# Layer 1's gate and up products by Strassen's algorithm, with one block of each pair run ahead for one half of the tokens

## The chip, the cores and the metric

One NeuronCore of a Trainium2 chip. TensorE (PE) multiplies, VectorE (DVE), ScalarE (ACT) and GpSimdE (POOL) work on tiles in on-chip memory, SyncE (SP) and ScalarE issue DMA transfers. The metric is the device time of one execution in microseconds. The kernel before: median 2474.93 us of 3 runs (2474.85 to 2480.22).

## The reference

A trunk of four residual layers over 1024 tokens of width 1024, in float32: a gMLP and pooling mixer, a SwiGLU ffn, RWKV-7 time mixing, a SwiGLU ffn, and a last norm. The change touches the last two:

```python
def wkv7_scan(r, w, k, v, a, b):        # 16 heads of 64 x 64 state, one step per token
    def step(state, inp):
        r_t, w_t, k_t, v_t, a_t, b_t = inp
        sa = jnp.einsum('bhvk,bhk->bhv', state, a_t)
        state = (state * w_t[:, :, None, :] + sa[..., None] * b_t[:, :, None, :]
                 + v_t[..., None] * k_t[:, :, None, :])
        return state, jnp.einsum('bhvk,bhk->bhv', state, r_t)

# in rwkv7_time_mix, on the scan's output y of each head:
mean = jnp.mean(y, axis=-1, keepdims=True)
var = jnp.mean(jnp.square(y - mean), axis=-1, keepdims=True)
y = ((y - mean) * lax.rsqrt(var + GN_EPS)).reshape(bsz, seq, d)
y = y * ln_w.astype(f32) + ln_b.astype(f32)
...
return (y * g) @ w_o, v_first

def swiglu(hn, w_gate, w_up, w_down):    # gate, up: 1024 x 2816, down: 2816 x 1024
    return (jax.nn.silu(hn @ w_gate) * (hn @ w_up)) @ w_down

h = h + swiglu(rms_norm(h, ffn_norm[layer]), ffn_w_gate[layer], ffn_w_up[layer], ffn_w_down[layer])
```

## The kernel before, in words

**Numbers.** A float32 matrix product is made of three float32r products of high and low parts: `mm3` issues hi x hi, lo x hi and hi x lo (lines 344 to 346) into one PSUM tile. Every dense matmul is 128x128 by 128x512. `split` makes the two parts: ScalarE copies to hi (line 143), VectorE subtracts for lo (line 144).

**Tiling.** Activations are transposed, features on partitions, in two halves of the tokens, A and B, of 512 each. The ffn's width of 2816 is 22 blocks of 128. For a block, gate and up take 8 steps of K times 3 matmuls each, 24, and so does down (8 output tiles). A unit of work in the text is 24 matmuls.

**Weights.** `push` writes the list of weight blocks (0.5 MB each) in the order of use; `take` hands out the next, and issues the load of the following ones on ScalarE's DMA queue into `raw` (3 tiles), and splits them into `whi` and `wlo` (3 tiles each).

**Order.** The Tile framework's scheduler sets the order of every engine's instructions from a timeline of its own; it is fixed when the program is built, and each engine then goes through its list in order. `drive(dense, side, ratio)` lets two generators of work go along: for each unit of the dense one the side one gets `ratio` of its own costs, at a priority that is `AHEAD` (450) instructions ahead. `beside` does the same for the projections.

**Layer 1.** For half A, then B: the projections (`project_gate`, `project`), the recurrence `recur(h)`, the output projection `out_proj`, the ffn. Recurrence (1), that of half B, runs beside the ffn of half A. `recur` goes through 8 chunks of 64 tokens. `burst` is one chunk: `below2` (sm<-XT,w), `own` (sm<-uv,gt, copied by ScalarE to akv), the product with the state (sm<-S,ar), the Gram products of the next chunk (`gram`, sm<-ar,bk, masked by VectorE to gt), sm<-Q,XT (copied to uv by ScalarE and VectorE), yp<-S,ar, sm<-uv,bkt with the new state S, yp<-uv,gt, then `flip_bk` of the next chunk (sm<-ident,bk, copied by ScalarE to bkt) and its `below` (sm<-XT,gt, copied by ScalarE and VectorE to w). bk has one tile, ar and uv two. `ordered` keeps the recurrence's TensorE instructions in the order written. After each second chunk `post` takes the pair's output yp: statistics (VectorE), rsqrt (GpSimd, line 349), 16 ScalarE instructions that scale yp into ysb, VectorE and GpSimd half each of the layer norm, eight transposes (sm<-ident,ysb) and eight VectorE products with the gate gch, which go to memory as y_d.

**What runs beside and after it.** `BESIDE` and `G1A` split half A's 22 ffn blocks: 2 beside `project_gate`, 16 (48 units with ratio 3.0) for recurrence (1), then 2 with the loads of y_d, the output projection of half B, `norm_split` of B (which makes B's normalised activations), the last 2 of A, and B's 22 blocks. `final_down` ends each half with the last norm and the transposes back.

## Time and profile before

| what | value |
|---|---|
| median of 3 runs | 2474.93 us (2474.85 to 2480.22) |
| profiled execution | 2477.63 us |
| its span, first to last instruction | 2475.9 us |
| TensorE busy | 2406.4 us, 97% |
| VectorE, ScalarE, GpSimd busy | 1382.7, 912.1, 244.6 us |
| DMA | 310.69 MB, mean 125 GB/s |
| recurrence (1) | about 1657 to 1870 us |
| half A's rest, y_d loads, output projection of B | 1870 to 2020 us |
| the rest of the ffn | 2020 to 2440 us |

Times inside an execution are microseconds from its first instruction. A group's row has line, engine, operation, output<-inputs by the program's names, shape and count, then busy time and mean nanoseconds of one, then the engine's idle time just before them with what ended most of it. PEld is the load of weights into TensorE, beside PE. Matmuls overlap, so their single durations add up to more than the time that they take. In a timeline a bracket gives the idle time ahead of an instruction and what released it.

### The profile page before, as it was taken

To read this page: it belongs to the slowest core of one execution; us is meant where nothing else is said; L and a number is where in the kernel's file an instruction comes from. 1 tells how busy PE (TensorE), PEld (TensorE's weight loads), DVE (VectorE), ACT (ScalarE), POOL (GpSimd) and SP (SyncE) were. 2 spreads that over 40 slices of the span, in tenths; PEclk is the share of its full clock that TensorE was granted. 3 is DMA by queue.
4 is the path that set the end of the run, shared out by engine and by line. 5 is a ranking of instruction groups with operands and counts; after the bars stand their busy time and mean duration, and the time that the engine had idled before them with its cause. 6 is when DMAs were issued, how large, how long until landed. Compare 5 with 4: busy or idle time off the path is not lost.

```text
span 2475.9 us, 37980 instructions
## 1 busy us (share of the span) xinstructions
PE 2406.4 (97%) x15735; PEld 1977.5 (80%) x15735; DVE 1382.7 (56%) x2126; ACT 912.1 (37%) x1369; POOL 244.6 (10%) x262
## 2 busy tenths in 40 slices
PE   8999999999999998999999999989999999999998
PEld 7888888888878787888878777778878778888887
DVE  6445634444875874655548847856555446444443
ACT  6233422222664432432325754433232324322223
POOL 0200000000014400211000133201111000000001
PEclk9999999999999999999999999999999999999999
DMA  5123433323355577542434465695444322433231
GB/s 179 49 60 89 150 102 102 119 86 94 109 176 139 140 208 202 156 127 70 135 112 143 153 168 134 191 234 140 119 128 128 111 85 75 147 102 118 87 98 56
DMA packets 436396, 310.69 MB, mean 125 GB/s; under 512 B 93376, under 2 KB 395584, under 8 KB 435456
## 3 DMA queue, kind: packets, MB, share of 16 engines
q10 hardware_dynamic: 297280, 210.53, 28.6%
q1 hardware_dynamic: 138944, 97.75, 13.8%
q8 instruction: 123, 2.02, 0.3%
q14 instruction: 49, 0.40, 0.1%
HBM read 254.68 MB, written 53.54 MB: 124 GB/s over the span
## 4 chain that ended last, share of the span: by engine, by line
PE 82%; DMA 6%; DVE 5%; ACT 2%; issue 2%; POOL 2%; SPq 0%; ACTq 0%; POOLq 0%; DVEq 0%
PE mm L344 22%; PE mm L345 22%; PE mm L346 22%; PE sm L1176 5%; DMA raw<-y_d 1%; DVE wlo L144 1%; PE yp L1176 1%; DMA raw<-in_ffn_w_down_dram 1%; DMA lnw<-in_rwkv_ln_w_dram 1%; ACT whi L143 1%; PE aux L1097 1%; PE mm L511 1%; PE mm L512 1%; PE mm L513 1%; PE aux L1098 1%
## 5 line engine op out<-in xcount | busy, mean ns | idle before, releaser
L345 PE MATMUL mm<-alo,whi 128*128 128x512 f32 x1952 | 766.7, 393 | 0.9 <-issue 0.8
L346 PE MATMUL mm<-ahi,wlo 128*128 128x512 f32 x1952 | 765.4, 392 | 1.7 <-DVE wlo L144 1.7
L344 PE MATMUL mm<-ahi,whi 128*128 128x512 f32 x1952 | 765.8, 393 | 0.8 <-ACT whi L143 0.8
L143 ACT ACTIVATE whi<-raw 128x1024 fp32r<-128x1024 f32 x288 | 304.6, 1059 | 744.7 <-PE mm L345 605.3
L144 DVE TENSOR_TENSOR wlo<-raw,whi 128x1024 fp32r<-128x1024 f32 x288 | 359.1, 1248 | 289.5 <-ACT whi L143 270.1
L346 PEld LDWEIGHTS mm<-ahi,wlo 128*128 128x128 f32 x1952 | 367.7, 188 | 82.5 <-issue 3.5
L345 PEld LDWEIGHTS mm<-alo,whi 128*128 128x128 f32 x1952 | 367.7, 188 | 79.9 <-issue 2.9
L344 PEld LDWEIGHTS mm<-ahi,whi 128*128 128x128 f32 x1952 | 367.7, 188 | 79.0 <-issue 2.1
L344 PE MATMUL mm<-hidhi,wdhi 128*128 128x512 f32 x624 | 240.5, 395 | 8.1 <-DVE h L424 3.8
L345 PE MATMUL mm<-hidlo,wdhi 128*128 128x512 f32 x624 | 245.0, 393 | 0.4 <-DVE hidlo L674 0.4
L346 PE MATMUL mm<-hidhi,wdlo 128*128 128x512 f32 x624 | 244.9, 392 | 0.0
L424 DVE TENSOR_TENSOR h<-h,mm 128x512 f32<-128x512 f32 x192 | 129.3, 686 | 149.7 <-PE mm L346 148.5
L143 ACT ACTIVATE wdhi<-raw 128x1024 fp32r<-128x1024 f32 x82 | 86.4, 1057 | 249.7 <-DMA raw<-in_ffn_w_down_dram 164.4
L144 DVE TENSOR_TENSOR wdlo<-raw,wdhi 128x1024 fp32r<-128x1024 f32 x82 | 100.2, 1223 | 112.1 <-ACT wdhi L143 112.0
L670 DVE TENSOR_TENSOR sg<-sg,mm 128x512 f32<-128x512 f32 x88 | 60.3, 686 | 157.1 <-PE mm L346 155.3
L344 PEld LDWEIGHTS mm<-hidhi,wdhi 128*128 128x128 f32 x624 | 117.5, 189 | 36.8 <-DVE h L424 6.4
L345 PEld LDWEIGHTS mm<-hidlo,wdhi 128*128 128x128 f32 x624 | 117.8, 189 | 25.7 <-DVE hidlo L674 1.3
L346 PEld LDWEIGHTS mm<-hidhi,wdlo 128*128 128x128 f32 x624 | 117.8, 189 | 24.9
L424 DVE TENSOR_TENSOR hA<-hA,mm 128x512 f32<-128x512 f32 x72 | 48.8, 686 | 77.2 <-PE mm L346 77.0
L349 POOL TENSOR_TENSOR nrs<-nrs,small 128x4 f32<-128x4 f32 x8 | 10.0, 1244 | 667.2 <-DVE nrs L371 667.2
L674 DVE TENSOR_TENSOR hidlo<-sg,hidhi 128x512 fp32r<-128x512 f32 x88 | 65.7, 748 | 10.0 <-ACT hidhi L673 10.0
L344 PE MATMUL mm<-xhi,whi 128*128 128x512 f32 (+1 forms) x160 | 65.3, 408 | 0.0
(299 smaller groups left out, 2886.3 us busy)
## 6 DMA issues: line engine op xcount, KB each, us to landing
raw<-in_ffn_w_gate_dram ACTq DMA_DIRECT2D x88, 512.0 KB
raw<-in_ffn_w_up_dram ACTq DMA_DIRECT2D x88, 512.0 KB
raw<-in_ffn_w_down_dram ACTq DMA_DIRECT2D x88, 512.0 KB
raw<-in_ab_w_in_dram ACTq DMA_DIRECT2D x16, 512.0 KB
raw<-in_ab_w_out_dram ACTq DMA_DIRECT2D x16, 512.0 KB
raw<-in_rwkv_w_r_dram ACTq DMA_DIRECT2D x16, 512.0 KB
raw<-in_rwkv_w_k_dram ACTq DMA_DIRECT2D x16, 512.0 KB
ar_d<-ar SPq DMA_DIRECT2D x16, 512.0 KB
```

The costliest lines, as they stand in the source:

```text
L143: act.activation(hi, src, AF.Copy)
L144: (eng or dve).tensor_tensor(out=lo, in0=src, in1=hi.bitcast(F32), op=ALU.subtract)
L344: pe.matmul(o, whi, xhi, start=first, stop=False)
L345: pe.matmul(o, whi, xlo, start=False, stop=False)
L346: pe.matmul(o, wlo, xhi, start=False, stop=last)
L424: dve.tensor_tensor(out=H[h][:, m, :], in0=H[h][:, m, :], in1=o, op=ALU.add)
L511: pe.matmul(ops[j], xhi[:, k, sl], whi[:, kk], start=(k == 0), stop=False)
L512: pe.matmul(ops[j], xhi[:, k, sl], wlo[:, kk], start=False, stop=False)
L513: pe.matmul(ops[j], xlo[:, k, sl], whi[:, kk], start=False, stop=(k == KT - 1))
L670: dve.tensor_tensor(out=s, in0=s, in1=o, op=ALU.mult)
L674: dve.tensor_tensor(out=lo, in0=s, in1=hi.bitcast(F32), op=ALU.subtract)
L1176: i = f(*args, **kw)
```

## The change

For layer 1's gate and up, a pair of column blocks (2i, 2i+1) with the two halves of K (rows of the weight) and the two halves of the tokens is a 2 x 2 by 2 x 2 block product. It is done with seven products of quarters where eight stood (Winograd's form of Strassen's algorithm); a quarter product is 4 steps of K, 12 matmuls. VectorE makes the sums of weights (`weights` in `full_steps`) and of activations (`combine`), and adds up the results.

- The even block of some pairs (0 to 20 in `AHEAD_OF`; here every pair has one) is done for half A ahead, as P1 + P2, its first product; P1 is kept in DRAM (`p1_d`). `ahead_steps` does gate, up and down of blocks 0, 2 beside `project_gate`, of 4, 6, 8, 10 for recurrence (1) with a ratio of 9.3 (12 units), of 12 and 14 with the loads of y_d. After B's output projection `first_steps` does gate and up of 16, 18, 20 (`FRONT`), beside `combine`, ratio 2.7.
- `full_steps` then does the other five quarter products of each of 11 pairs, for gate and up. The hidden values go to DRAM (`hid_d`), and so does the residual of both halves (`hz_d`).
- `down_steps` does the rest of down, half A's 14 blocks and then half B's 22, with the hidden tiles loaded back.
- In `recur`, `post` copies yp to ysb on ScalarE first and goes on from there; the eight transposes and what follows (`turn_out`) are issued one chunk later, after the next `flip_bk`, and for the last pair at the end.
- `final_down` makes its first transposes after its first products.

```diff
-BESIDE = (4, 2)
+BESIDE = 4
+PAIRS = 11
+AHEAD_OF = ([0, 2],), ([4, 6], [8, 10]), ([12, 14],), (16, 18, 20)
...
+    def ahead_events(groups):
+        for gi, g in enumerate(groups):
+            for f in g:
+                if gi == 0 or f != g[0]:
+                    yield "gu", f
+            if gi + 1 < len(groups):
+                yield "gu", groups[gi + 1][0]
+            yield "d", g
...
+    FRONT = [(f // 2, f, n, True) for f in AHEAD_OF[3] for n in range(2)]
+    for i, f, n, _ in FRONT:
+        push(("first", f, n), push_pair(1, i, n, f % 2))
+    for i, n in mats(range(PAIRS)):
+        for j in range(2):
+            push((f"full{j}", i, n), push_pair(1, i, n, j))
...
+    def first_steps(blocks, hn, fp):
+        b11, b21 = (parts_of(hn, slice(k, k + 4)) for k in (0, 4))
+        sg, prev = {}, []
+        def second(i, f, n, w, o):
+            quarter(o, parts_of(w, HI), b21, False)
+            if n == 0:
+                sg[f] = fp.tile([P, HT], F32, tag="t2", bufs=2, name="sg")
+                act.activation(sg[f], o, AF.Silu)
+            else:
+                s = sg.pop(f)
+                dve.tensor_tensor(out=s, in0=s, in1=o, op=ALU.mult)
+                save_hidden(fp, 0, f, s)
+        for i, f, n, kept in blocks:
+            w = take(("first", f, n))
+            o = mmt()
+            quarter(o, parts_of(w, LO), b11, True)
+            if kept:
+                t = fp.tile([P, HT], F32, tag="t1", bufs=2, name="p1")
+                act.activation(t, o, AF.Copy)
+                sp.dma_start(p1_d[:, 2 * i + n, :], t)
+            yield 0.5
+            if prev:
+                second(*prev.pop())
+                yield 0.5
+            prev.append((i, f, n, w, o))
+        second(*prev.pop())
...
+            if kind == "gu":
+                b11, b21 = (parts_of(hn, slice(k, k + 4)) for k in (0, 4))
+                w, os_ = [take((k, 1, 0, f)) for k in "gu"], [mmt(), mmt()]
+                for n in range(2):
+                    yield from quarter_steps(os_[n], parts_of(w[n], LO), b11, True)
+                    t = fp.tile([P, HT], F32, tag="p1", bufs=2 if nd else 1, name="p1")
+                    act.activation(t, os_[n], AF.Copy)
+                    sp.dma_start(p1_d[:, f + n, :], t)
+                for n in range(2):
+                    yield from quarter_steps(os_[n], parts_of(w[n], HI), b21, False)
+                    if n == 0:
+                        s = fp.tile([P, HT], F32, tag="sg", bufs=2, name="sg")
+                        act.activation(s, os_[n], AF.Silu)
+                    else:
+                        dve.tensor_tensor(out=s, in0=s, in1=os_[n], op=ALU.mult)
+                        hid[f] = [fp.tile([P, HT], F32R, tag=t, bufs=nh, name=t) for t in ("hidhi", "hidlo")]
+                        split(s, *hid[f])
...
+    def full_steps(blocks, kept, x, fp, wp):
+        sub = ALU.subtract
+        def weights(i):
+            (a11, a12), (a21, a22) = ((raws[j][:, LO], raws[j][:, HI]) for j in (i - 1, i))
+            s3 = wp.tile([P, HT], F32, tag="s3", bufs=1, name="s3")
+            dve.tensor_tensor(out=s3, in0=a11, in1=a21, op=sub)
+            s1, s2, s4 = a21, a11, a12
+            dve.tensor_tensor(out=s1, in0=a21, in1=a22, op=ALU.add)
+            dve.tensor_tensor(out=s2, in0=s1, in1=a11, op=sub)
+            b = whl()
+            split(s2, *parts_of(b, HI))
+            split(s1, *parts_of(b, LO))
+            d = [wp.tile([P, HT], F32R, tag=t, bufs=1, name=t) for t in ("s3hi", "s3lo")]
+            split(s3, *d)
+            dve.tensor_tensor(out=s4, in0=a12, in1=s2, op=sub)
+            c = [wp.tile([P, D], F32R, tag=t, bufs=2, name=t) for t in ("chi", "clo")]
+            split(a22, *parts_of(c, LO))
+            split(s4, *parts_of(c, HI))
+            return b, c, d
...
+        for i, n in blocks:
+            k = i in kept
+            a = mmt()
+            w = take(("full0", i, n))
+            if not k:
+                quarter(a, parts_of(w, LO), x["b11"], True)
+                t1 = tile_("t1")
+                act.activation(t1, a, AF.Copy)
+                yield 0.5
+                o = mmt()
+                quarter(o, parts_of(w, HI), x["b21"], True)
+                dve.tensor_tensor(out=t1, in0=t1, in1=o, op=ALU.add)
+                finish(i, n, 0, t1)
+                yield 0.5
+            b, c, d = take(("full1", i, n))
+            quarter(a, parts_of(b, HI), x["t2"], k)
+            yield 0.5
+            if prev:
+                prev[0]()
+                yield 0.5
+            if k:
+                t1 = tile_("t1")
+                sp.dma_start(t1, p1_d[:, 2 * i + n, :])
+            def now(t, k=k, a=a, t1=t1):
+                if k:
+                    dve.tensor_tensor(out=t, in0=t1, in1=a, op=ALU.add)
+                else:
+                    act.activation(t, a, AF.Copy)
+            u2, u3 = tile_("t2"), tile_("t3")
+            now(u2)
+            o = mmt()
+            quarter(o, parts_of(b, LO), x["t1"], True)
+            yield 0.5
+            if prev:
+                prev[1]()
+                yield 0.5
+            quarter(a, d, x["t3"], False)
+            now(u3)
+            dve.tensor_tensor(out=u3, in0=u3, in1=o, op=ALU.add)
+            finish(i, n, 3, u3)
+            yield 0.5
+            def last(i=i, n=n, k=k, a=a, t1=t1, c=c, now=now):
+                quarter(a, parts_of(c, LO), x["t4"], False)
+                if k:
+                    now(t1)
+                    finish(i, n, 2, t1)
+                else:
+                    finish(i, n, 2, tile_("t4"), a)
+            def last2(i=i, n=n, o=o, u2=u2, c=c):
+                quarter(o, parts_of(c, HI), x["b22"], False)
+                dve.tensor_tensor(out=u2, in0=u2, in1=o, op=ALU.add)
+                finish(i, n, 1, u2)
+            prev = last, last2
...
+        def prime(n=1):
+            for g in groups[:n]:
+                load(g)
+        def steps():
+            for gi, g in enumerate(groups):
+                load(g)
+                wd = {f: take(("d", l, h, f)) for f in g}
+                if gi in at:
+                    at[gi]()
+                if ahead and gi + 1 < len(groups):
+                    load(groups[gi + 1])
...
                 bkt = flip_bk(c + 1)
+                if turned:
+                    turned.pop()()
...
+            ysb = wt("ysb", 1, [P, 2, 8, 64])
+            for r in range(2):
+                act.activation(ysb[:, r], ypair[0][:, r], AF.Copy)
...
-                    dve.bn_stats(out=st[:, r, p, :], in_=yp[:, r, p, :])
+                    dve.bn_stats(out=st[:, r, p, :], in_=ysb[:, r, p, :])
...
+            def turn_out():
+                for q in range(2):
+                    o = pst("sm")
+                    for i in range(4):
+                        p = 4 * q + i // 2 * 2
+                        ordered(
+                            pe.transpose, o[:, i * P : (i + 1) * P],
+                            ysb[:, i % 2, p : p + 2, :].rearrange("t p d -> t (p d)"), ident,
+                        )
...
+            turned.append(turn_out)
...
+        turned.pop()()
+        yield 1.0
...
-    drive(ffn(1, 0, hnA, f, G1A[1]), with_reload(hp, 0, h_d[0, 1], recur(1, wp)), RATIO)
+    drive(ahead_steps(AHEAD_OF[1], hnA, f, 2, 3), with_reload(hp, 0, h_d[0, 1], recur(1, wp)), 9.3)
...
+    drive(ahead_steps(AHEAD_OF[2], hnA, f, 2, 3, lambda m: sp.dma_start(hz_d[0][:, m, :], H[0][:, m, :]), take_act(("y", 1))))
...
+    exhaust(out_proj(1, ys, after))
...
+    def combine(bc_):
+        sub = ALU.subtract
+        def new():
+            return rp.tile([P, HT], F32, tag="rt", bufs=3, name="rt")
+        def keep(t, to, k):
+            split(t, *(y[:, k, :] for y in x[to]))
+        for k in range(4):
+            b12, b22 = (nt.tile([P, HT], F32, tag="nsq", bufs=2, name="hn") for _ in range(2))
+            for m, t in ((k, b12), (k + 4, b22)):
+                dve.scalar_tensor_tensor(
+                    out=t, in0=H[1][:, m, :], scalar=col(C_FFN + 8 + m), in1=bc_, op0=ALU.mult, op1=ALU.mult
+                )
+            (b11h, b11l), (b21h, b21l) = ([y[:, k, :].bitcast(F32) for y in x[n]] for n in ("b11", "b21"))
+            keep(b22, "b22", k)
+            yield 1.0
+            t1 = new()
+            dve.tensor_tensor(out=t1, in0=b12, in1=b11h, op=sub)
+            dve.tensor_tensor(out=t1, in0=t1, in1=b11l, op=sub)
+            keep(t1, "t1", k)
+            yield 1.0
+            t2 = new()
+            dve.tensor_tensor(out=t2, in0=b22, in1=t1, op=sub)
+            keep(t2, "t2", k)
+            t3 = new()
+            dve.tensor_tensor(out=t3, in0=b22, in1=b12, op=sub)
+            keep(t3, "t3", k)
+            yield 1.0
+            t4 = new()
+            dve.tensor_tensor(out=t4, in0=b21h, in1=t2, op=sub)
+            dve.tensor_tensor(out=t4, in0=t4, in1=b21l, op=ALU.add)
+            keep(t4, "t4", k)
+            yield 1.0
+    drive(first_steps(FRONT, hnA, f), combine(norm_bcast(acc[0])), 2.7)
...
+    exhaust(full_steps(mats(range(PAIRS)), range(PAIRS), x, f, wp))
...
+    prime_b, steps_b = down_steps(1, 1, D1B, wslot, hslot, last=True)
+    prime_a, steps_a = down_steps(
+        1, 0, D1A, lambda f: lw if f == one else wslot(f), lambda f: low[:, 4:6, :] if f == one else hslot(f),
+        at={len(D1A) - 1: prime_b}, last=True,
+    )
+    prime_a(2)
+    reload(hb_pool, 1, hz_d[1])
     fgb = fin_pool.tile([P, D], F32, name="fgb")
     act.dma_start(fgb, final_norm.partition_broadcast(P))
-    reload(hb_pool, 1, h_d[1, 1])
-    ys = open_act(("y", 1), b)
-    drive(ffn(1, 0, hnA, f, G1A[2], between=take_act(("y", 1))))
-    exhaust(out_proj(1, ys))
-    hnB = norm_split(1, C_FFN + 8, b)
-    drive(ffn(1, 0, hnA, f, G1A[3], last=True))
-    drive(ffn(1, 1, hnB, f, last=True))
-    for e in (fin_es, hb_es, b_es, hp_es, nxt["a_es"], f_es, ps_es):
+    drive(steps_a)
+    drive(steps_b)
```

TensorE in recurrence (1), before: its last chunk, with sm the PSUM tile of the recurrence, L1176 its matmuls, and hid and wd the hidden values and weights of down.

```order
L1176 MATMUL sm<-ident,bk 128x128 x8
L1176 MATMUL sm<-XT,gt 32x32 x16
L345 MATMUL mm<-alo,whi 128x512
...
L346 MATMUL mm<-ahi,wlo 128x512
...
L1176 MATMUL sm<-S,ar 64x64 x16
L346 MATMUL mm<-hidhi,wdlo 128x512
...
L1176 MATMUL yp<-S,ar 64x64 x16
L344 MATMUL mm<-hidhi,wdhi 128x512
...
L1176 MATMUL sm<-ident,ysb 128x128 x7
L344 MATMUL mm<-ahi,whi 128x512
```

The same place now, to the end of the recurrence and the first dense rows behind it (L1498 is the recurrence, L770 to 772 `quarter_steps` of block 12).

```order
L1498 MATMUL sm<-ident,bk 128x128 x8
L1498 MATMUL sm<-ident,ysb 128x128 x8
L1498 MATMUL sm<-XT,gt 32x32 x16
...
L1498 MATMUL sm<-S,ar 64x64 x16
L1498 MATMUL sm<-Q,XT 64x64 x16
L1498 MATMUL yp<-S,ar 64x64 x16
L1498 MATMUL yp<-uv,gt 64x64 x16
L1498 MATMUL sm<-ident,ysb 128x128 x8
L770 MATMUL mm<-ahi,whi 128x512
L771 MATMUL mm<-alo,whi 128x512
```

The dense rows between the recurrence's steps are gone here: from the middle of chunk 4 on, 575 matmuls of the recurrence follow each other, and the last pair's transposes stand ahead of the next dense row.

VectorE at the end of `combine` and ahead of the first full product; L155 is the lo part of `split`, L820 to L829 the sums of weights of the first block, xlo the lo parts of the combined activations.

```order
L1978 TENSOR_TENSOR rt<-hn 128x512
L155 TENSOR_TENSOR alo<-rt,ahi 128x512
L155 TENSOR_TENSOR xlo<-rt,xhi 128x512
L1982 TENSOR_TENSOR rt<-ahi,rt 128x512
L155 TENSOR_TENSOR xlo<-rt,xhi 128x512
L1983 TENSOR_TENSOR rt<-rt,alo 128x512
L155 TENSOR_TENSOR xlo<-rt,xhi 128x512
L820 TENSOR_TENSOR s_17279<-raw 128x512
L155 TENSOR_TENSOR clo<-raw,chi 128x512
L822 TENSOR_TENSOR raw<-raw 128x512
```

All of `combine` (60 rows from the first hn on, with three wlo of FRONT among them) stands ahead of the first pair's weights; before, `norm_split` of half B stood at this place, with a norm product and a lo part for each of 8 tiles.

SyncE around the switch to down: hz_d_79 is half B's h, hid_d the hidden values, hd their tiles.

```order
L733 DMA hid_d_76<-hid 128x1024 x2
L1807 DMA h<-hz_d_79 128x4096
L733 DMA hid_d_75<-hid 128x1024
L733 DMA hid_d_76<-hid 128x1024
L931 DMA hd<-hid_d_75 128x1024 x13
```

The reload of half B's h and the last two saves stand ahead of the first hidden tiles; this queue did neither before.

More of the change, by code (lines that the diff above doesn't have):

```diff
@@ L1365, in post @@
             yield 0.3
-            ysb = wt("ysb", 1, [P, 2, 8, 64])
             for r in range(2):
@@ L1444, in final_down @@
             products(1, 0)
+            turned = turned or [turn(h, j) for j in range(4)]
             for j in range(4):
@@ L1566, in blocks @@
         yield from out_proj(0, ys, sums_a)
-        yield from ffn(1, 0, hnA, f, G1A[0], nd=2, after=spill_a)
+        yield from ahead_steps(AHEAD_OF[0], hnA, f, 0, 2, after=spill_a)
     def norm_a():
         hnA.extend(norm_split(0, C_FFN + 8, y, n_d[1], norm_bcast(sums)))
-    beside(1, blocks(), [1] * 8 + weights_of(G1A[0]), parts, (8, norm_a))
+    weights = [2 if kind == "gu" else len(g) for kind, g in ahead_events(AHEAD_OF[0])]
+    beside(1, blocks(), [1] * 8 + weights, parts, (8, norm_a))
     for e in (f_es, y_es, hb_es, ps_es):
```

211 lines of the change are left out of this document (181 added, 30 removed).

## The prediction

> **What bounds the kernel now.** I read the profile's head first, then the costliest groups, then TensorE by stage, then its waits.
>
> ```profile
> span 2475.9 us, 37980 instructions
> PE 2406.4 (97%) x15735; PEld 1977.5 (80%) x15735; DVE 1382.7 (56%) x2126; ACT 912.1 (37%) x1369; POOL 244.6 (10%) x262
> L345 PE MATMUL mm<-alo,whi 128*128 128x512 f32 x1952 | 766.7, 393 | 0.9 <-issue 0.8
> L144 DVE TENSOR_TENSOR wlo<-raw,whi 128x1024 fp32r<-128x1024 f32 x288 | 359.1, 1248 | 289.5 <-ACT whi L143 270.1
> L424 DVE TENSOR_TENSOR h<-h,mm 128x512 f32<-128x512 f32 x192 | 129.3, 686 | 149.7 <-PE mm L346 148.5
> ```
>
> TensorE is busy 97% of the span. Its matmuls overlap, so the 393 ns of one is no price. The price is in the windows by stage (columns: window, length, busy time and count of PE, PEld, DVE, ACT, POOL, granted clock, DMA share, GB/s):
>
> ```profile
> 1640.00:1655.00 15.00, 11.08 (x75) 8.55 (x74) 4.34 (x5) 3.64 (x5) 0.00 (x0) 1.00 1.10 271
> 1655.00:1660.00 5.00, 2.44 (x37) 2.04 (x38) 3.62 (x5) 1.88 (x3) 0.00 (x0) 0.62 1.10 346
> 1660.00:1665.00 5.00, 5.00 (x17) 3.97 (x17) 1.74 (x3) 2.51 (x4) 0.00 (x0) 0.70 1.17 251
> 1665.00:1870.00 205.00, 199.75 (x3007) 166.71 (x3006) 117.09 (x248) 62.94 (x124) 30.13 (x26) 0.99 0.43 123
> 1870.00:1945.00 75.00, 75.00 (x336) 62.09 (x335) 35.33 (x45) 25.54 (x42) 5.18 (x3) 1.00 0.44 139
> 1945.00:2020.00 75.00, 69.52 (x289) 55.32 (x288) 35.47 (x44) 18.97 (x23) 0.00 (x0) 0.95 0.37 114
> 2020.00:2440.00 420.00, 420.00 (x1876) 347.68 (x1875) 191.79 (x231) 124.22 (x167) 8.60 (x9) 1.00 0.32 98
> 2150.00:2200.00 50.00, 50.00 (x222) 41.40 (x221) 20.13 (x23) 12.37 (x15) 0.00 (x0) 1.00 0.31 95
> ```
>
> In a stage without waits 222 matmuls of 128x512 take 50.00 us: **0.2252 us each**, 5.41 for a unit of 24. From 2020 to 2440 TensorE is never idle, though VectorE is at 46% and DMA at 98 GB/s. So less matmul work there is worth its full price as long as the rest keeps up. The recurrence of layer 1 idles only 5.25 us of the 205 from 1665 to 1870, because dense matmuls stand between its steps.
>
> **What is removed.** Each engine's rows in program order, counted: TensorE has 12345 dense matmuls where it had 12609, all 128x512, so 264 fewer. 264 x 0.2252 = **-59.5**. Nothing else leaves TensorE's path; the rows are issued or not, so that part cannot fail to happen. Weight loads of gate and up fall from 176 to 154, off the path before and now.
>
> **The end of the recurrence.** Before, recurrence (1) had 48 dense units of 24 matmuls to draw on; now it has 12. The order of TensorE puts all 288 dense matmuls ahead of chunk 4's middle and then 575 matmuls of the recurrence in a row, ending with the eight transposes of the last ysb. What a bare chunk takes is read in the timeline of before (start, length, engine):
>
> ```profile
> 1739.23 0.69 PE L1176 MATMUL sm<-XT,w 32*32 32x32 f32 x32
> 1749.50 1.09 PE L1176 MATMUL sm<-ident,bk 128*128 128x128 f32 x8
> 1751.23 0.69 PE L1176 MATMUL sm<-XT,gt 32*32 32x32 f32 x32
> 1751.97 0.38 ACT L1249 ACTIVATE w<-sm 32x256 f32<-32x256 f32 x1 [0.69 <-PE sm L1176]
> 1752.56 0.43 DVE L1250 COPY w<-sm 32x256 f32<-32x256 f32 x1
> 1745.78 0.59 ACT L1293 ACTIVATE uv<-sm 64x512 f32<-64x512 f32 x1 [4.14 <-PE sm L1176]
> ```
>
> From XT,w to the end of the bk transposes are 11.36 us, some 1.8 of it dense; with XT,gt 10.2 of TensorE. The copies of w (1751.92 to 1752.99) now have nothing beside them, 1.1 us a chunk, and at most some 2.5 if the reload of bk's single buffer (0.5 MB, priced as the load of 3.7 below) is later than they are: 3.4 chunks, 4 to 8.5 us, I take 6. The last pair's outcome is dearer, since the transposes wait for all of it and nothing dense may pass them:
>
> ```profile
> 1864.55 2.20 DVE L1353 BATCH_NORM_STATS2 st<-yp 128x6 f32<-128x64 f32 x16 [2.69 <-PE yp L1176]
> 1868.83 2.91 POOL L349 TENSOR_TENSOR var<-var,small 128x16 f32<-128x16 f32 x1 [34.89 <-DVE var L1362]
> 1872.05 4.84 ACT L1370 ACTIVATE ysb<-yp,mean,var 128x64 f32<-128x64 f32 x16 [13.48 <-DVE mean L1364]
> 1876.96 1.29 POOL L1375 TENSOR_TENSOR ysb<-ysb,lnw 128x512 f32<-128x512 f32 x1 [5.22 <-ACT ysb L1370]
> 1878.33 2.15 POOL L1376 TENSOR_TENSOR ysb<-ysb,vch 128x512 f32<-128x512 f32 x1
> 1750.19 1.09 ACT L1234 ACTIVATE bkt<-sm 128x512 f32<-128x512 f32 x2 [3.82 <-PE sm L1176]
> ```
>
> 1864.55 to 1880.48 is 15.9; the added pair of copies (priced by bkt) is 1.1 more, and an h of 1.28 that stood between on VectorE is gone: **15.9 us idle**. Before, dense work of 1870 to 1945 covered this. For the pair before it ScalarE's queue holds the uv copy of the next chunk behind 16 ysb: ysb end some 12.3 us after yp, where a bare chunk wants uv 9.5 after, so 2.8 late. That happens in chunks 4 and 6; TensorE waits for uv, and so does the next state: 0 to 6, I take 4. Of the 5.25 idle now, some 2 belong to chunks that no longer have it. 15.9 + 6 + 4 - 2 = **+24** (15 to 29).
>
> **The combinations of the activations.** `combine` needs b, which TensorE makes after 59 of FRONT's 144 matmuls; 85 remain, 19.1 us of cover. VectorE has 60 instructions after b and before the first pair's weights: 8 scalar-tensor-tensors, 3 wlo, 49 of 128x512. Then come five more before the first full product can start. VectorE's pace when it is never idle:
>
> ```profile
> 699.58 0.68 DVE L670 TENSOR_TENSOR sg<-sg,mm 128x512 f32<-128x512 f32 x1
> 709.32 0.75 DVE L883 SCALAR_TENSOR_TENSOR mix<-hn,vec,mix 128x512 f32<-128x512 f32 x1
> 711.84 1.23 DVE L144 TENSOR_TENSOR wlo<-raw,whi 128x1024 fp32r<-128x1024 f32 x1
> ```
>
> From the start of the first row to that of the last are 19 instructions in 12.26 us, one of them another wlo of 1.23: 0.61 for a 128x512. So at least 62 x 0.61 + 3 x 1.23 - 19.1 = 22.4; by the means of single rows (0.69, 0.75, 1.25) 43.5 + 3.5 - 19.1 = 27.9, more where VectorE waits for ScalarE's hi part. I take **+27**, near the means, as these chains alternate engines. The next thing late is the raw tiles of the second block, which the first block's own operations free: one load, whose price is here:
>
> ```profile
> 1952.96 0.39 ACTq L113 DMA_DIRECT2D raw<-in_ffn_w_up_dram  x1
> 1956.67 1.06 ACT L143 ACTIVATE whi<-raw 128x1024 fp32r<-128x1024 f32 x1 [3.52 <-DMA raw<-in_ffn_w_up_dram]
> ```
>
> 3.7 us from issue to use: **+4** once (0 to 8).
>
> **The loop of 11 pairs.** A pair (gate and up) is 120 matmuls, 27.0 us. VectorE has 34 instructions for it, 20.7 at 0.61 and 23.9 by the means of single rows: under TensorE, but by little. Of each pair's four raw loads the second of the up block is issued after the gate block's last clo; s3hi and s3lo have one buffer. Nothing waits if there is a block's lead: 0. If that load is bare, 23.9 + 3.7 = 27.6, 0.6 a pair; two bare, 31.3 and 47 in all. I take 0.9 a pair, **+10** (0 to 47), near one bare load. Saves and reloads of P1 and of the hidden values (0.25 and 0.5 MB) ride beside it: 98 GB/s is used where 271 is to be had.
>
> **The start of down.** SyncE's queue issues the reload of half B's h (2 MB) and two saves ahead of the hidden tiles of the second group; TensorE has one group of 24 matmuls as cover, 5.4 us. At 271 GB/s 2 + 1 + 1.5 MB are 16.6 us, so 11 late if they go strictly in turn, 3 if the tiles overtake. **+8**, with the switch to half B. Later groups need about 1 MB per 5.4 us, 190 GB/s, which the first windows above exceed.
>
> **The clock.** After the one long idle of before the matmuls ran slow:
>
> ```profile
> 1657.57 1.11 PE L1176 MATMUL sm<-ident,bk 128*128 128x128 f32 x4 [4.58 <-DVE gt L1223]
> 1658.61 1.06 PE L1176 MATMUL sm<-XT,gt 32*32 32x32 f32 x32
> 1660.20 0.63 PE L344 MATMUL mm<-ahi,whi 128*128 128x512 f32 x1
> 1663.12 0.39 PE L345 MATMUL mm<-alo,whi 128*128 128x512 f32 x1
> ```
>
> Matmuls 0.43 apart until 1663 against 0.225, so about 1.6 us for each restart. Three long idles: **+5** (0 to 8).
>
> The output projection, its loads and the last turns stay (idle there, 5.5 from 1945 to 2020, is left in). Sum: -59.5 + 24 + 27 + 4 + 10 + 8 + 5 = **+18.5**, a span of 2494.4. The profiled execution took 2477.63, 1.7 more than its span; the median of the runs is 2474.93, 2.7 under it. So the median is forecast at **2493**.
>
> **Rivals.** *VectorE runs back to back* (faster): at 0.61 an instruction FRONT's gap is 23, the pair needs 21 of 27 us and never shows; the uv copies are in time (recurrence +20), down +3, clock +2: -59.5 + 20 + 23 + 3 + 2 = -11.5, **2463.5**. For it: the 12 us stretch above. Against: wlo waits 289.5 us for ScalarE in all, so such stretches are short. It decides from where a pair's VectorE work with its waits is under 27.0.
>
> *The raw slot binds every pair* (slower still): two loads bare, +47 for 10: **2530**. For it: three raw tiles, all four loads of a pair chained to VectorE's last use. Against: from 2020 to 2440 TensorE never waits with the same three raw tiles, and one of the two loads can be issued a block earlier.
>
> *The bare recurrence loses the clock.* Its 3.4 chunks have 35 us of TensorE work in small matmuls with a gap or more in each; if these ran as at 1658.61 (XT,gt 1.06 for 0.69) or as ident,bk (4 in the time of 8), they take 1.5 to 2 times as long, +17 to +35: **2519**. Against: the granted clock is 0.99 from 1665 to 1870 with the same small matmuls, though dense ones stand between. The Trainium skill ("TensorE: Matmul & The Clock Gate", "A second HAM failure mode: psum-queue depth-cycling") says that frequent short idles between groups of matmuls can make the gate swing between half and full rate; its section "HAM oscillation" asks for an idle above some 3.4 us. By the first rule this rival holds, by the second the forecast; no run here shows a bare chunk yet.
>
> **Chances.** Forecast 0.46, its own range 2483 to 2508 (the terms' errors against each other; 0.05 of it within 0.3%). VectorE back to back 0.32, of which 0.20 faster by over 0.3% and 0.12 within (waits a little above their least). Raw slot 0.16, clock 0.06, both slower. 0.3%, about 7.4 us, is what a measurement here can tell from no change. Together faster 0.20, same 0.17, slower 0.63. The range 2462 to 2534 leaves out half of the first rival's faster part and the worst of the raw slot.
>
> **What would show it.** In the new trace: TensorE idle some 16 us ahead of the last transposes of ysb, released by VectorE or GpSimd; idle of 23 to 28 us ahead of the first product of x after FRONT, released by wlo, with VectorE full; in the loop 120 matmuls in 27 to 29 us and VectorE at 75 to 88%; a wait of 3 to 11 us for hd at the start of down. The forecast is wrong if the first two gaps are together under 30 us, if the loop takes over 31 us a pair, or if the bare chunks show a clock near 0.5.

## The result: slower by 1.8%, and the profile after

The changed kernel takes 2522.24 us (median of 4 runs, 2518.19 to 2524.18) where the kernel before takes 2477.55 (2474.85 to 2480.22): a ratio of 1.0178, interval 1.0158 to 1.0199. Forecast was slower by 18.5 us; it is slower by 44.7. The direction and the range held, the size did not. The profiled execution took 2518.19 us, 1.7 more than its span, so it lies 4 under the median.

The head of the page of the kernel after:

```profile
span 2516.5 us, 38279 instructions
PE 2373.7 (94%) x15471; PEld 1944.6 (77%) x15471; DVE 1515.6 (60%) x2413; ACT 946.4 (38%) x1464; POOL 239.7 (10%) x262
```

264 instructions of TensorE are gone, as counted. At 0.2252 us each its busy time should have fallen by 59.5; it fell by 32.7. Its idle time, span less busy, rose from 69.5 to 142.8, by 73.3. So the loss has two parts: 73.3 of idle, and 26.8 (59.5 less 32.7) of matmuls that were busy longer.

Those of TensorE's waits in the kernel after that bear on the sum (engine, line, tile, what it waited for: total, times, longest):

```profile
PE mm L720 <- ACT whi L154: 24.2, 1, 24.2
PE sm L1498 <- DVE uv L1616: 13.1, 3, 4.9
PE sm L1498 <- DVE ysb L1703: 11.5, 1, 11.5
PE mm L396 <- DMA hd<-hid_d: 8.2, 1, 8.2
PE sm L1498 <- DVE gt L1545: 7.3, 8, 3.9
PE mm L720 <- ACT s3hi L154: 4.9, 10, 0.5
PE mm L770 <- ACT p L787: 4.7, 5, 2.8
PE sm L1498 <- POOL ysb L1703: 3.3, 1, 3.3
```

The first row is the wait ahead of the first full product, the two of ysb are the bare end of recurrence (1), hd is the start of down, s3hi the loop. Of the others over 3.5 us, one of 6.1 (for vrow) and those for a, 3.8 together, have their like in the kernel before (6.0 and 4.8); one of 4.8 for sg just ahead of recurrence (1) stands where the kernel before waits 4.6 for gt.

To place the loss I split each execution at the same events, and take from the length of each stretch 0.2252 us for each matmul of 128x512 recorded in it. What remains is the stretch's other matmuls, idle time and slow clock; it doesn't matter how much dense work the scheduler put there. The windows for the two recurrences and for what follows, before and then after (window, length, PE busy with count, PEld, DVE, ACT, POOL, granted clock, DMA share, GB/s):

```profile
951.50:1178.40 226.90, 224.15 (x3175) 187.48 (x3176) 130.08 (x265) 76.43 (x152) 37.02 (x28) 0.99 0.44 125
1657.50:1885.60 228.10, 222.79 (x3131) 185.68 (x3132) 129.11 (x264) 75.34 (x151) 35.30 (x28) 0.98 0.44 122
```

```profile
955.00:1180.20 225.20, 213.67 (x3097) 178.11 (x3098) 122.08 (x259) 77.05 (x154) 33.26 (x28) 0.95 0.43 122
1677.40:1836.50 159.10, 129.52 (x2702) 111.64 (x2701) 92.30 (x228) 59.29 (x132) 34.58 (x28) 0.89 0.42 124
1945.00:1985.00 40.00, 15.84 (x63) 12.62 (x62) 37.32 (x61) 17.10 (x28) 0.00 (x0) 0.70 0.40 140
1985.00:2265.00 280.00, 275.06 (x1202) 224.53 (x1201) 211.86 (x336) 95.45 (x159) 0.00 (x0) 1.00 0.48 147
2265.00:2320.00 55.00, 45.26 (x191) 36.34 (x190) 33.34 (x48) 12.87 (x18) 0.00 (x0) 0.94 0.66 242
```

| stretch, time beyond its dense matmuls (us) | before | after | more |
|---|---|---|---|
| up to recurrence (0) | 108.4 | 111.9 | 3.5 |
| recurrence (0) | 94.7 | 109.7 | 15.0 |
| between the recurrences | 78.7 | 83.5 | 4.8 |
| recurrence (1) | 98.6 | 126.2 | 27.6 |
| from there to the end | 30.5 | 79.6 | 49.1 |
| sum | 410.9 | 510.9 | 100.0 |

100.0 - 59.5 = 40.5, and the spans differ by 40.6. The part to the end, 49.1, is mostly 25.8 in the 40 us around the start of the full products, 9.3 in the loop's 280, and 12.0 in the 55 around the start of down. Recurrence (0), far from layer 1's ffn, lost 15.0: that is the surprise, and the prediction has nothing for it.

### The profile page after: what moved, and what is told of

It reads as the page before. It is cut to its first block, busy times and chain, and to the rows that moved or that the text cites. A ratio compares the mean times of both kernels' runs of the same rounds, so it can differ in the third digit from the quotient of the medians.

```text
span 2516.5 us, 38279 instructions
## 1 busy us (share of the span) xinstructions
PE 2373.7 (94%) x15471; PEld 1944.6 (77%) x15471; DVE 1515.6 (60%) x2413; ACT 946.4 (38%) x1464; POOL 239.7 (10%) x262
## 3 DMA queue, kind: packets, MB, share of 16 engines
q8 instruction: 121, 1.98, 0.3%
## 5 line engine op out<-in xcount | busy, mean ns | idle before, releaser
L397 PE MATMUL mm<-alo,whi 128*128 128x512 f32 x1248 | 491.2, 394 | 0.0
L396 PE MATMUL mm<-ahi,whi 128*128 128x512 f32 x1248 | 490.6, 393 | 0.0
L398 PE MATMUL mm<-ahi,wlo 128*128 128x512 f32 x1248 | 490.1, 393 | 0.4 <-DVE wlo L155 0.4
L154 ACT ACTIVATE whi<-raw 128x1024 fp32r<-128x1024 f32 (+1 forms) x267 | 263.1, 986 | 598.5 <-PE mm L397 427.2
L155 DVE TENSOR_TENSOR wlo<-raw,whi 128x1024 fp32r<-128x1024 f32 (+1 forms) x267 | 307.4, 1152 | 208.6 <-ACT whi L154 189.3
L398 PEld LDWEIGHTS mm<-ahi,wlo 128*128 128x128 f32 x1248 | 235.2, 188 | 52.1 <-issue 2.3
L397 PEld LDWEIGHTS mm<-alo,whi 128*128 128x128 f32 x1248 | 235.3, 189 | 50.7 <-issue 2.5
L396 PEld LDWEIGHTS mm<-ahi,whi 128*128 128x128 f32 x1248 | 235.2, 188 | 49.9 <-issue 1.8
L398 PE MATMUL mm<-hidhi,wdlo 128*128 128x512 f32 x368 | 144.4, 392 | 0.0
L396 PE MATMUL mm<-hd,dhi 128*128 128x512 f32 x248 | 97.3, 393 | 12.6 <-DMA hd<-hid_d 8.2
L155 DVE TENSOR_TENSOR wdlo<-raw,wdhi 128x1024 fp32r<-128x1024 f32 x46 | 57.5, 1254 | 79.0 <-ACT wdhi L154 79.0
L397 PE MATMUL mm<-hd,dhi 128*128 128x512 f32 x248 | 97.0, 391 | 0.0
```

The source lines that it names most:

```text
L154: act.activation(hi, src, AF.Copy)
L155: (eng or dve).tensor_tensor(out=lo, in0=src, in1=hi.bitcast(F32), op=ALU.subtract)
L396: pe.matmul(o, whi, xhi, start=first, stop=False)
L397: pe.matmul(o, whi, xlo, start=False, stop=False)
L398: pe.matmul(o, wlo, xhi, start=False, stop=last)
```

## Experiments

Numbers are medians, and the ratio to the kernel before of the same comparison, with its interval; stretches are as in the table, each read from one profiled execution. The change itself stands at 1.0178 (1.0158 to 1.0199). The kernel before took 2479.0 to 2479.8 in these comparisons, and an interval reaches some 4 to 5 us to either side, so a difference of that size between two variants is not shown.

### The recurrence edit alone, and undone

**The edit alone** in the kernel before: `burst` and `post` of `recur` from the change.

```diff
                 bkt = flip_bk(c + 1)
+                if turned:
+                    turned.pop()()
...
+            ysb = wt("ysb", 1, [P, 2, 8, 64])
+            for r in range(2):
+                act.activation(ysb[:, r], ypair[0][:, r], AF.Copy)
...
+            turned.append(turn_out)
```

> The kernel before with the change's recurrence alone (copy of yp to ysb, transposes one chunk later, in both recurrences). Theory 1 (the recurrence edit itself costs time where dense work is plentiful, because the copies and the 16 scalings hold ScalarE's queue, which also issues the weight loads and makes uv): slower than before by 12 to 30 us, TensorE waiting for uv in recurrence (0) for some 8 us, granted clock below 1 behind these waits. Theory 2 (dense work covers it, and the loss of the change lies in layer 1 alone): within 5 us of before.

2489.05 us, 1.0041 (1.0026 to 1.0057): slower by about 10, under the range of theory 1, with its signs. Recurrence (0) has 106.1 beyond its dense matmuls (94.7 before), with two waits for uv, 7.1 us together. Recurrence (1) has 94.0 (98.6): there, under as much dense work, the same edit gains 4.6.

**The edit undone** in the changed kernel: `recur` as in the kernel before.

> The changed kernel with the recurrence as it was before (statistics and scaling from yp, transposes in the same chunk). Theory 1: 12 to 25 us faster than the change, the idle and slow clock of recurrence (0) gone, the bare end of recurrence (1) still there. Theory 2: within 4 us of the change.

2520.31 us, 1.0161 (1.0142 to 1.0180): 2 us from the change. That is theory 2's number, but not its reason, as the windows tell:

```profile
955.30:1183.90 228.60, 226.34 (x3175) 189.18 (x3176) 130.53 (x265) 76.43 (x152) 36.36 (x28) 0.98 0.44 123
1666.00:1836.00 170.00, 126.10 (x2701) 109.17 (x2700) 91.62 (x226) 53.30 (x124) 33.89 (x28) 0.85 0.40 114
```

Recurrence (0) is back at 96.4, 13 better. Recurrence (1) idles 43.9 of 170 us, 14 more than with the edit, and has 137.3 for 126.2: without dense work beside it, the old order waits for each pair's outcome before it may go on. So the edit costs 11 to 15 in recurrence (0), and in recurrence (1) it gains 11 without cover and 4.6 with it: the amount of dense work alone does not decide. It was applied to both.

**Its two parts.** First the copy alone:

```diff
-            yp = ypair[0]
+            ysb = wt("ysb", 1, [P, 2, 8, 64])
+            for r in range(2):
+                act.activation(ysb[:, r], ypair[0][:, r], AF.Copy)
...
-                    dve.bn_stats(out=st[:, r, p, :], in_=yp[:, r, p, :])
+                    dve.bn_stats(out=st[:, r, p, :], in_=ysb[:, r, p, :])
```

> The kernel before with only the copy of yp to ysb (statistics and scaling go on from the copy); the transposes stay in their chunk. Theory 1 (the copies, with the 16 scalings, hold ScalarE's queue, so weight loads and uv come late): 6 to 14 us slower than before, nearly all of what the whole recurrence edit cost there (10). Theory 2 (the later transposes do it): within 4 us of before.

2489.15 us, 1.0043 (1.0026 to 1.0059). By the time theory 1 holds; by the place it does not: recurrence (0) has 96.4 and (1) 97.6, nearly as before. In its profile (6 us over that of before; its execution was the fastest of the four, 6 under their median) the loss is behind recurrence (1), 37.2 for 30.5, where TensorE waits 7.4 for hidhi instead of 3.3. How the copy leads there I did not find out.

Then the later transposes alone, with statistics and scaling from yp:

```diff
                 bkt = flip_bk(c + 1)
+                if turned:
+                    turned.pop()()
...
+            turned.append(turn_out)
```

> The kernel before with only the transposes one chunk later (statistics and scaling from yp as before). Theory 1: within 4 us of before. Theory 2: 6 to 14 us slower.

2499.32 us, 1.0082 (1.0067 to 1.0097): slower by 20, twice the whole edit and beyond theory 2's range. Recurrence (0) has 112.3 and (1) 103.9. So theory 2 holds for the place: the later transposes are what hurts the recurrences. The parts don't add up (10 and 20, together 10), so with the copy part of this comes back; how is not shown.

**What waits there.** ScalarE's timeline in recurrence (0) of the changed kernel:

```profile
1009.88 1.06 ACT L154 ACTIVATE whi<-raw 128x1024 fp32r<-128x1024 f32 x1 [1.29 <-PE mm L397]
1010.85 0.62 ACT L995 ACTIVATE hidhi<-sg 128x512 fp32r<-128x512 f32 x1
1012.24 0.35 ACTq L118 DMA_DIRECT2D raw<-in_ffn_w_down_dram  x1
1018.51 1.06 ACT L154 ACTIVATE wdhi<-raw 128x1024 fp32r<-128x1024 f32 x1 [7.04 <-DMA raw<-in_ffn_w_down_dram]
1019.47 0.57 ACT L1615 ACTIVATE uv<-sm 64x512 f32<-64x512 f32 x1
```

and TensorE, the last matmuls of uv's product and those that wait for uv:

```profile
1014.76 0.22 PE L1498 MATMUL sm<-Q,XT 64*64 64x64 f32 x1
1021.61 1.98 PE L1498 MATMUL sm<-uv,bkt 128*64 128x64 f32 x32 [3.91 <-DVE uv L1616]
```

ScalarE stands 7 us before wdhi, whose raw tile ScalarE itself asked for only at 1012.24. uv's product was done at 1015, but uv has its place behind wdhi. The 32 matmuls then take 1.98 us where the same took 1.15 at 992.40: the clock has fallen too, to 0.50 from 1022 to 1026. The same row of waits in three kernels, over recurrence (0): before, then the later transposes alone, then the change:

```profile
ACT wdhi L143 <- DMA raw<-in_ffn_w_down_dram: 13.9, 6, 5.5
```

```profile
ACT wdhi L143 <- DMA raw<-in_ffn_w_down_dram: 22.5, 6, 6.4
```

```profile
ACT wdhi L154 <- DMA raw<-in_ffn_w_down_dram: 28.9, 6, 7.0
```

ScalarE always waited for these loads; with the later transposes it waits longer, and with uv behind it. Why the load of 1012.24 went out so late was not tested; VectorE had just finished reading a raw tile (wlo, 1010.98 to 1012.21), which may be the one that it needed. The test is to take ScalarE out of uv's path:

```diff
-            act.activation(uv[rows[0], :, 0, :], ou[rows[0]], AF.Copy)
+            dve.tensor_copy(uv[rows[0], :, 0, :], ou[rows[0]])
```

> The changed kernel with both halves of the uv copy on VectorE (ScalarE had one). Theory 1 (uv waits in ScalarE's queue, behind a weight's hi part whose load has not landed in recurrence (0), behind the 16 scalings in recurrence (1)): TensorE's three waits for uv, 13.1 us, go, and part of the slow clock behind them: 8 to 18 us faster than the change. Theory 2 (something ahead of uv is late): within 4 us.

2508.51 us, 1.0119 (1.0100 to 1.0139): 14 faster than the change; TensorE's waits for uv fall from 13.1 us to 2.0. In recurrence (0) they fall from 8.8 to 0.3, though ScalarE still stands 18.9 us for wdhi there, up to 7.0 at a time; only uv is no longer behind it. Recurrence (0) falls from 109.7 to 99.9, two thirds of what it had lost. Recurrence (1) stays (125.3), though its uv waits fall there too, from 4.3 to 1.7. Theory 1 holds, for recurrence (0). Of the 14 the traces show 4.8: their executions were the slowest of the four here and the fastest of the change, and between the recurrences this kernel has 5.3 more.

### Cover moved within layer 1

**More dense work beside recurrence (1), less beside the combinations.**

```diff
-AHEAD_OF = ([0, 2],), ([4, 6], [8, 10]), ([12, 14],), (16, 18, 20)
+AHEAD_OF = ([0, 2],), ([4, 6], [8, 10], [12, 14]), ([16, 18],), (20,)
```

> The changed kernel with blocks 12 and 14 beside recurrence (1) (18 units for 12), 16 and 18 with the loads of y_d, and only 20 in FRONT. TensorE's order then has 124 matmuls of the recurrence in a row at its end where there were 575. Theory 1 (a bare chunk costs idle and clock, beyond the cover that is missing): recurrence (1) loses 25 to 30 us less, the wait for the combinations grows by 18 to 22, so 5 to 12 us faster than the change. Theory 2 (cover is only moved from one wait to another): within 4 us of the change.

2521.13 us, 1.0171 (1.0152 to 1.0191): 1 us from the change. (The order of down's last groups and the ratio, 6.2 for 9.3, go with it.) Recurrence (1) gains 11.0 (115.2). The wait ahead of the full products, which lost 96 matmuls of cover, 21.6 us, grows by 13.2, to 37.4:

```profile
PE mm L720 <- ACT whi L154: 37.4, 1, 37.4
```

Theory 2 by the time: cover is moved, not made. Both changes are smaller than theory 1 had them.

**The same dense work kept for the end of recurrence (1).** One matmul in `burst` makes the scheduler do so.

```diff
                 w1 = below(c + 1)
+                if h == 1 and c >= 4:
+                    fill(1)
```

> The changed kernel with one matmul of 128x512 added in each of chunks 4 to 6 of recurrence (1), whose result goes nowhere; it makes the scheduler keep the same 288 dense matmuls for the end: 808 matmuls of the recurrence in a row early, and some 30 dense ones ahead of the last transposes. Theory 1 (a bare chunk costs little beside the bare end): the wait of 14.8 us ahead of the last transposes falls by 6 to 7, 4 to 10 us faster than the change. Theory 2 (bare chunks cost as much wherever they are, by idle and by a granted clock that falls in them): within 4 us of the change, with a clock under 0.9 in the early bare stretch.

2527.79 us, 1.0193 (1.0174 to 1.0212): 5.6 above the change by the medians, 3.7 by the ratios, and the intervals overlap, so a loss is not shown; theory 1's gain is ruled out. The wait for the last ysb falls from 14.8 to 10.8, but recurrence (1) as a whole has 135.6 for 126.2. So the bare stretch cost at least what its move took off the end, and theory 2 is the nearer one. The granted clock was 0.66 in 1730 to 1740 and 0.83 in 1750 to 1760 of it, 1.00 in most of the rest, so theory 2's sign is there too.

**The clock in a bare chunk** is best seen in the changed kernel itself: two windows, then every wait of TensorE in the second.

```profile
1780.00:1790.00 10.00, 9.13 (x292) 8.59 (x293) 6.41 (x13) 1.71 (x5) 0.61 (x2) 1.00 0.54 153
1790.00:1800.00 10.00, 7.80 (x180) 6.88 (x180) 4.97 (x27) 5.89 (x15) 2.91 (x1) 0.72 0.44 139
```

```profile
1792.38 0.24 PE L1498 MATMUL sm<-XT,w 32*32 32x32 f32 x2 [0.84 <-ACT w L1571]
1793.13 0.69 PE L1498 MATMUL sm<-XT,w 32*32 32x32 f32 x30 [0.51 <-DVE w L1572]
1796.98 0.71 PE L1498 MATMUL sm<-ar,bk 64*64 64x128 f32 x8 [0.49 <-DMA bk<-bk_d]
1798.05 1.56 PE L1498 MATMUL sm<-ar,bk 64*64 64x128 f32 x24 [0.36 <-issue]
```

No wait is longer than 0.84 us, and still the clock falls to 0.72: the 24 matmuls at 1798 take 1.56 us, where 27 of the same took 0.99 at 1688.56. The Trainium skill ("TensorE: Matmul & The Clock Gate") has two rules for this. Its section "HAM oscillation" asks for an idle above some 3.4 us, and there is none here. "A second HAM failure mode: psum-queue depth-cycling" says that frequent short idles between groups of matmuls do it, and these rows agree. They don't single out the idles, though: the window ahead has waits of 0.53 and 0.81 us too and kept 1.00. No run here changes the clock alone, so what tips it stays open.

### The combinations

**Without T3 and T4**, so with 20 VectorE instructions fewer.

```diff
-            t3 = new()
-            dve.tensor_tensor(out=t3, in0=b22, in1=b12, op=sub)
-            keep(t3, "t3", k)
...
-            keep(t4, "t4", k)
```

> The changed kernel without the combinations T3 and T4 (left out; the products with them take T2 in their place): 20 VectorE instructions fewer ahead of the first full product. Theory 1 (VectorE's queue sets the wait there): the wait of 24 us ahead of the first full product falls by 20 x 0.62 to 0.69, 12 to 14 us, and the time with it. Theory 2 (the first pair's weights, their loads or ScalarE set it): the wait stays above 20 us.

2507.81 us, 1.0113 (1.0095 to 1.0130): 14 faster than the change. TensorE's idle time from 1945 to 1985 falls from 24.2 to 11.6, by 12.6, 0.63 us an instruction:

```profile
1945.00:1985.00 40.00, 28.43 (x116) 22.45 (x115) 32.14 (x52) 15.81 (x26) 0.00 (x0) 0.87 0.49 163
```

Theory 1: VectorE's queue sets this wait. (Eight copies to hi parts on ScalarE are gone as well; ScalarE was busy 8.65 of the 20 us from 1960 to 1980.)

**A part of them on GpSimd.**

```diff
-            dve.tensor_tensor(out=t1, in0=b12, in1=b11h, op=sub)
-            dve.tensor_tensor(out=t1, in0=t1, in1=b11l, op=sub)
+            pool.tensor_tensor(out=t1, in0=b12, in1=b11h, op=sub)
+            pool.tensor_tensor(out=t1, in0=t1, in1=b11l, op=sub)
+            keep(t1, "t1", k, pool)
...
```

> The changed kernel with 16 of the instructions of the combinations (the two subtractions of T1 and the lo parts of T1 and B22, four of each) on GpSimd instead of VectorE. Theory 1 (VectorE's queue alone sets the wait ahead of the first full product): the wait falls from 24 to some 13 us and the time by 8 to 12. Theory 2 (the chain T1, T2, T4 sets it, and GpSimd at 1.3 us an instruction makes it longer): the wait stays above 20 us or grows.

2526.8 us, 1.0192 (1.0177 to 1.0207): 5 above the change by the medians, 3.5 by the ratios, with intervals that overlap; certainly not the gain of theory 1. The wait is still 21.3, and a second one stands 26 us ahead of it:

```profile
PE mm L720 <- ACT whi L154: 21.3, 1, 21.3
PE mm L720 <- ACT p L756: 5.1, 1, 5.1
```

Together they are 26.4, more than the 24.2 of the change: ScalarE, which copies p, itself waited 4.1 and 1.5 us there for sums that VectorE made. Theory 2's number holds, but not for the chain: VectorE is full. From 1960 to 1980, in the change and then with GpSimd:

```profile
1960.00:1980.00 20.00, 1.43 (x3) 1.16 (x4) 19.17 (x32) 8.65 (x14) 0.00 (x0) 0.50 0.45 161
```

```profile
1960.00:1980.00 20.00, 0.65 (x3) 0.16 (x1) 18.15 (x24) 7.71 (x13) 9.08 (x6) 0.59 0.34 115
```

32 VectorE instructions in the change, 24 with GpSimd beside them, at nearly the same busy time. One group of each, from 1945 to 1980:

```profile
L1983 DVE TENSOR_TENSOR rt<-rt,alo 128x512 f32<-128x512 f32 x4 | 2.7, 681 | 0.0
```

```profile
L1983 DVE TENSOR_TENSOR rt<-rt,alo 128x512 f32<-128x512 f32 x4 | 6.0, 1490 | 0.0
```

An instruction that takes 0.68 us alone takes 1.49 beside GpSimd, in the mean of four. The Trainium skill ("SBUF — State Buffer", section "Who interferes with whom") says that a VectorE instruction with two inputs in SBUF and a GpSimd instruction that reads SBUF keep each other out; this case agrees: GpSimd's own took 1.28 us at the least, and in the mean of a group 1.4 to 1.9.

### Versions made from this

Fewer pairs leave whole blocks: half A's ahead, as cover, and half B's as P1 + A11 T1 + A12 B22 behind FRONT, where they cover the making of T2 to T4. The recurrence edit is kept for (1) alone, and half B's h comes after the first hidden tiles.

```diff
-PAIRS = 11
-AHEAD_OF = ([0, 2],), ([4, 6], [8, 10]), ([12, 14],), (16, 18, 20)
+PAIRS = 9
+AHEAD_OF = ([0, 2],), ([4, 6], [8, 10], [12, 14], [16]), ([18],), (19, 20, 21)
+SINGLE = list(range(2 * PAIRS, 22))
...
+    drive(single_steps(SINGLE, x, f), combine2(), 1.5)
```

> A version made from the findings: 9 pairs by Strassen, blocks 18 to 21 done whole (half A ahead, half B as P1 + A11 T1 + A12 B22), so 21 units beside recurrence (1) for 12; T1 and B22 made first and T2 to T4 beside the whole blocks of half B; half B's h reloaded behind the first hidden tiles; recurrence (0) as before. 48 matmuls more than the change, 216 fewer than before, -48.6 us. Theory (cover and VectorE's queue explain the loss): the bare chunks and the wait for the combinations are gone, what is left is the loop's 4 to 5, 3 to 6 at the start of down, and up to 8 of slow clock: 2440 to 2465, faster than both. Rival (the scheme itself loses what it saves): 2475 or more.

2481.82 us, 1.0011 (1.0001 to 1.0020): the rival. The wait for the combinations is down to 3.6, but recurrence (1) still has 109.8, with 9.2 us bare at its end. With 24 units beside it, and the down of the block that covers the loads of y_d put behind the output projection:

```diff
-AHEAD_OF = ([0, 2],), ([4, 6], [8, 10], [12, 14], [16]), ([18],), (19, 20, 21)
+AHEAD_OF = ([0, 2],), ([4, 6], [8, 10], [12, 14], [16, 18]), ([19],), (20, 21)
...
+    exhaust(rest)
```

> The nine pairs again with 24 units beside recurrence (1) where the first such version had 21, the down of the block that covers the loads of y_d put behind the output projection, and two blocks in FRONT for three. Theory (what nine pairs still lost were the bare end of recurrence (1), 9 us and its clock, and a block whose down waits for its own gate, 7 us): 2458 to 2472. Rival (the combinations' wait comes back with the shorter FRONT): 2475 or more.

2474.18 us, 0.9974 (0.9963 to 0.9984). Recurrence (1) has 102.9. It misses the theory's range by 2 us.

```diff
-PAIRS = 9
-AHEAD_OF = ([0, 2],), ([4, 6], [8, 10], [12, 14], [16, 18]), ([19],), (20, 21)
+PAIRS = 8
+AHEAD_OF = ([0, 2],), ([4, 6], [8, 10], [12, 14], [16, 17]), ([18],), (19, 20, 21)
```

> The same with eight pairs (24 matmuls more, 5.4 us), so FRONT has three blocks again and six blocks are done whole. Theory: no wait for the combinations, 2460 to 2472; against the nine pairs it tells what a longer cover is worth. Rival: 5 us behind the nine pairs, as the matmuls alone make it.

2469.95 us, 0.9970 (0.9955 to 0.9986), in the theory's range: faster than both kernels, by 0.3% and 2.1%. Recurrence (0) has 94.5, (1) 102.1, TensorE is never idle from 1945 to 1975, where the combinations are made; from recurrence (1) to the end it has 57.4 beyond its dense matmuls where the kernel before has 30.5. Of its 43.2 us of matmuls saved over three quarters are given back. The interval of the nine pairs overlaps its own, so eight against nine is open.

## Why the prediction was wrong in size

**Right, by its steps.** -59.5 of matmuls: 264 gone, and the table closes with them. (The 12609 and 12345 of the prediction can't all be 128x512, as they would fill 2840 us; the traces hold 9184 and 8920 of 512 columns, with the same difference.) The end of recurrence (1), +24: TensorE's idle time there went from 5.3 to 29.6, +24.3. Of it the bare end was 14.8 (11.5 for VectorE's half of ysb and 3.3 for GpSimd's) against 15.9; the waits for w 4.0 against 6; uv 4.3 against 4; 3.5 more were for p, ScalarE's copy of P1, which the sum did not have, so the total is closer than its parts. The combinations, +27: 24.2 idle, 25.8 with the restart. The loop and its start, +14: 4.9 idle, s3hi (one buffer) ten times half a microsecond, and no bare load, by which the prediction had priced it. The start of down, +8: 9.7 idle, of it 8.2 for hd. All idle terms together, 73, against 73.3 measured, which is luck: 8.8 of idle in recurrence (0), which was not among them, stand in for the 9 by which the loop and its start were set too high. So the 22 us by which the span's 40.6 exceed the forecast's 18.5 all stand in matmuls that were busy longer, 26.8 for the +5 of the clock.

**The step that failed** is the one on the recurrence: "The end of the recurrence" costed the edit of `post` in recurrence (1) alone. The same code is recurrence (0), and there it cost 15.0 us, 8.8 of them idle and the rest slower matmuls (11.4 alone in the kernel before, 13 when undone). The prediction said "Before, dense work of 1870 to 1945 covered this" and took dense work as cover for everything; in recurrence (0) dense work is plentiful, and what was late is ScalarE, whose one queue issues the weight loads, splits the weights and copies uv; with uv taken out of it 9.8 of the 15.0 go. The prediction shows no row of ScalarE's order there.

**The second is a term of the wrong size**, the clock: +5 was put down for three restarts after long idles. Weighted with TensorE's busy time in windows of 4 us, the time lost to a granted clock under 1 went from 21.5 to 43.6 us, +22: 5 in recurrence (1), 6 in recurrence (0), behind its waits for uv, 3 behind recurrence (1), and 8 before and between the recurrences. The rival on the clock had the right place, and the clock did fall there, but not its size: it was 0.75 on average from 1765 to 1837, not a half throughout. Its 2519 came near by luck, for a sum that was not this one. The last 8 are nearly all of the 8.3 that the table has there, since idle did not grow (48.0 before, 46.7 after). Ahead of recurrence (0) they come and go: 12.6 are lost to the clock in the change, 5.8 in the kernel with uv on VectorE, with the same matmuls, and 5.8 in the kernel before. Between the recurrences every kernel made from the change has 83.5 to 88.8, where the kernel before and those with the recurrence edit alone or in parts have 77.5 to 80.4; what the change costs there stays open.

The other rivals: VectorE back to back held in the loop (211.86 us busy in 280, TensorE idle 4.9) and at the combinations (0.63 an instruction), but these terms were too small to turn the sign. The raw slot never held TensorE in the loop, though VectorE waited 31.5 us there for raw loads.

**Still open** is why later transposes alone hurt more than with the copy; their waits are spread over gt, uv, bkt, XT and Q. Also where the copy alone loses its time, and whether another engine's queue for the loads would mend recurrence (0).

## What to carry to other kernels

When a helper is edited, cost the edit at every place that calls it, and read the order of the engine that issues loads there: here an instruction that waited for a late load of its own queue held all that stood behind it, 7.0 us at a time. Dense work that hides waits is a stock; taking matmuls out of it, or moving it from one wait to another, showed up elsewhere here (11.0 gained, 13.2 lost), so count the waits that it still has to cover before counting the matmuls saved. Here eight of eleven pairs, with the rest done plainly as cover, beat both kernels, the one before by 0.3%.

## What the runs showed of the hardware

The clock granted to TensorE fell to 0.72 in a stretch of small matmuls whose idle gaps were at most 0.84 us. A window of 10 us just ahead, with idle gaps of up to 0.81 us, kept 1.00. VectorE instructions with two inputs took a mean of 1.49 us in place of 0.68 while GpSimd worked on tiles beside it; with 16 of them moved to GpSimd TensorE's idle time there was 26.4 us for 24.2. ScalarE stood up to 7.0 us for a weight load that its own queue had asked for 6.3 us earlier, with an unrelated copy behind it.
